# Group B's decoded attention: operands held as plain fp32, values computed with 64 stationary columns of one key head

## The chip, the cores and the metric

The kernel runs on one core of one Trainium2 chip. The metric is the device time of one execution in microseconds (us). The time before is 2622.76 us, the median of three runs (2622.56 to 2625.93).

The engines are named as in the profile: PE is TensorE, the matrix engine (PEld its weight loads), DVE VectorE, ACT ScalarE, POOL GpSimd, SP SyncE, which here only issues transfers. "L207" is line 207 of the kernel.

## The reference

One layer of an encoder that serves a prompt of 512 frames and, in the same step, 8 decoded sequences (batches) of 16 new frames each. The normed input goes through one combined projection, whose columns belong to two groups of attention heads, A and B. The change touches group B of the decoded batches, and nothing else. Cut to that:

```python
DEC_BATCH, DEC_SEQ, HEAD_DIM = 8, 16, 64
N_HEADS_B, N_KV_B, GQA_R, B_WINDOW = 16, 2, 8, 128

def band_attend(q, k, v, valid, bias=None, sink=None):
    s = jnp.einsum('bgqhrd,bgkhd->bghrqk', q, k) * (HEAD_DIM ** -0.5)
    ...
    m = jnp.max(s, axis=-1, keepdims=True)
    m = jnp.maximum(m, sink)
    p = jnp.exp(s - m)
    denom = jnp.sum(p, axis=-1, keepdims=True) + jnp.exp(sink - m)
    o = jnp.einsum('bghrqk,bgkhd->bgqhrd', p / denom, v)
    ...

def sample_layer(x, ck_a, cv_a, ck_b, cv_b, ...):
    ...
    ob = band_attend(qb.reshape(b, 1, s, N_KV_B, GQA_R, HEAD_DIM),
                     jnp.concatenate([ck_b, kb], axis=1)[:, None],
                     jnp.concatenate([cv_b, vb], axis=1)[:, None],
                     jnp.ones((1, keep_b + s), dtype=bool), sink=sinks.reshape(N_KV_B, GQA_R))
```

For each batch there are 16 query heads over 2 key heads (8 query heads to each), 16 query frames, and 128 cached keys with 16 new ones behind them. So for one batch and one key head the scores are a matrix of 128 (8 heads times 16 frames) by 144 (128 cached and 16 new keys), with 64 numbers summed in each product; the values are 128 by 64, summed over 144 keys. Each row of the scores goes through a softmax with a sink, an extra term in the denominator.

## The kernel before, in words

**Precision.** The output is compared in fp32. A large product is computed as three matmuls in the fp32r format (`mm3`, lines 207 to 209): each operand is split into a rounded part hi and the rest lo, and hi·hi, hi·lo and lo·hi are summed in one bank of PSUM. `split` makes the two parts: ScalarE rounds (line 198), VectorE subtracts (line 199). Small products, as the reciprocal norm's broadcast (line 263), are single matmuls in plain fp32. One such matmul stands in the profile as two PE instructions.

**The stream of projections.** `dense` computes a block of 128 output features for 640 frames: for each of 16 feature tiles of the input, and each half of 320 frames, one `mm3` into a bank named `dn`. In the trace these are the rows "L207 PE MATMUL dn<-S,W 128x320" and so on; they run nearly all the time. Their weights come in by SP's queue (line 219) and are split by ScalarE and VectorE as tiles W of 128 by 1024.

**Attention is woven in.** Attention is written as generators (functions with `yield`). After each feature tile `dense` calls `tick` (line 96), which adds `rate` to a counter and for each whole one runs one piece, up to the next `yield`, of the streams in turn. From the fifth pair of heads on the two streams are the prompt's heads of group A and "decode", and the rate is 1.1. "decode" holds `decode_b` (group B, this change), and after it `decode_a(0)` (half of group A). The scheduler then orders each engine's instructions by when it expects them to be ready; a few constraints keep the order of the projections, of the slots' uses and of some pieces. So what a piece issues stands among projection matmuls, and how many stand between two pieces is the scheduler's choice.

**Memory slots.** Tiles on chip take slots from lists: S (62 slots), W (12), and D, 10 slots set aside for decoding. A slot's next user waits for its last reader. PSUM holds four `bank()` tiles (named `at`), which prompt and decode share.

**`decode_b` before (lines 584 to 644).** Queries and keys lie with features on the partitions: rows 0 to 63 belong to key head 0, rows 64 to 127 to key head 1. For each half of four batches:
- it loads cached keys, cached values and this half's queries into three S slots (lines 589 to 591). The queries come from a DRAM scratch `sb_d`, written after rotation (rope, lines 560 and 561 its four small transfers for each tile);
- it splits queries, keys and values into six D slots, and POOL copies the 16 new keys of each batch, hi and lo, behind the cached ones (line 600);
- for each batch, and for each of the two key heads, an `mm3` on the key head's 64 rows gives the scores, 128 by 144, in a bank. The softmax follows: VectorE's row maximum (615), the sink (616), POOL's memset (619), ScalarE's exponentials (620, 621), and VectorE's denominator, reciprocal and products (622 to 625), which give the probabilities: 128 for the cached keys and 128 for all batches' new keys, zero but for this batch's 16;
- after two yields `flip` transposes the four blocks of probabilities (line 324, four matmuls into one bank) and splits the bank into two S slots;
- one piece later two `mm3` of 128 stationary columns (both key heads' values) by 256 moving columns (both key heads' probabilities) give the values, the first against the cache, the second against the new frames `vb_own`, kept as hi and lo. Of the 128 by 256 result two quarters of 64 by 128 are wanted; VectorE copies them (line 638).

Then the result is written out, and `decode_a(0)` takes its turn.

## Time and profile before

| what | value |
|---|---|
| median of three runs | 2622.76 us |
| span of the profiled execution, first to last instruction | 2619.7 us |
| what stands outside that span, against the median | 3.1 us |
| mean granted clock of TensorE | 0.997 |
| busy, PE / VectorE / ScalarE / POOL | 2565.2 / 2027.7 / 1101.9 / 663.8 us |
| `decode_b` on TensorE, first scores to last values | about 405 to 480 us |

Busy time is the sum over an engine's instructions. A matmul's record overlaps that of the next one, so the cost of one is read from start to start. A row of the timeline gives the start, the duration, engine, line, operation and tiles, the number of instructions run together, and in brackets how long the engine waited and for what. A group's row gives the busy sum and the mean in ns of one, then the idle time ahead of it. A window's row gives the window, its length, the busy time (and count) of PE, PEld, VectorE, ScalarE and POOL, the granted clock, the share of the transfers and GB/s.

### The profile page before, as it was taken

How to read it: one execution, taken by the hardware profiler on the slowest of the kernel's cores; microseconds unless marked ns; L12 is line 12 of the kernel's file. 1: busy time of each engine (PE TensorE's matmuls, PEld its weight loads, DVE VectorE, ACT ScalarE, POOL GpSimd, SP SyncE). 2: the span in 40 equal slices, each digit the busy share in tenths (PEclk: the TensorE clock that was granted, in tenths of full speed). 3: DMA queues.
4: the chain of work that ended last, by engine and by line, in shares of the span. 5: the costliest groups of instructions: out<-in, count | busy, mean ns of one | idle time of the engine just before them, and what ended most of it. 6: DMA issues, size and time to landing. Idle time of an engine off the chain costs nothing.

```text
span 2619.7 us, 45100 instructions
## 1 busy us (share of the span) xinstructions
PE 2565.2 (98%) x17437; PEld 2527.9 (96%) x17437; DVE 2027.7 (77%) x3133; ACT 1101.9 (42%) x1797; POOL 663.8 (25%) x573
## 2 busy tenths in 40 slices
PE   8999999999999999999999999999999899999997
PEld 8999998999899999999999999999999899999996
DVE  5775676766866888788888888888888877777797
ACT  5553444444633644443433333433434333333343
POOL 0000000000301203332333333323324433333353
PEclk9999999999999999999999999999999999999998
DMA  5322232444655433443343343343445865666655
GB/s 172 101 69 91 94 102 86 133 124 130 214 188 185 155 131 122 160 162 126 131 142 126 130 144 123 131 146 120 133 147 176 280 189 157 175 175 169 192 156 176
DMA packets 178678, 383.87 MB, mean 147 GB/s; under 512 B 21856, under 2 KB 74080, under 8 KB 178464
## 3 DMA queue, kind: packets, MB, share of 16 engines
q1 hardware_dynamic: 154128, 326.92, 38.8%
q0 software_dynamic: 23184, 52.77, 7.1%
q8 instruction: 137, 2.24, 0.3%
q10 hardware_dynamic: 1152, 1.31, 0.1%
q14 instruction: 77, 0.63, 0.1%
HBM read 299.61 MB, written 80.58 MB: 145 GB/s over the span
## 4 chain that ended last, share of the span: by engine, by line
PE 85%; DVE 8%; DMA 3%; ACT 2%; issue 2%; POOL 0%; SPq 0%; DVEq 0%; ACTq 0%; POOLq 0%
PE dn L209 18%; PE dn L207 18%; PE dn L208 18%; PE at L207 9%; PE at L208 9%; PE at L209 9%; DVE W L199 2%; PE at L324 2%; DMA W<-w_down 1%; PE at L419 1%; DVE S L973 1%; ACT W L198 1%; PE at L215 1%; PE at L214 1%; ACT S L440 0%
## 5 line engine op out<-in xcount | busy, mean ns | idle before, releaser
L207 PE MATMUL dn<-S,W 128*128 128x320 f32 x3694 | 1152.5, 312 | 5.2 <-ACT S L1027 2.7
L209 PE MATMUL dn<-S,W 128*128 128x320 f32 x3694 | 1144.5, 310 | 6.7 <-DVE W L199 6.3
L208 PE MATMUL dn<-S,W 128*128 128x320 f32 x3694 | 1143.3, 310 | 2.0 <-DVE S L203 1.7
L198 ACT ACTIVATE W<-W 128x1024 fp32r<-128x1024 f32 (+2 forms) x632 | 608.2, 963 | 965.9 <-PE dn L208 542.8
L199 DVE TENSOR_TENSOR W<-W,W 128x1024 fp32r<-128x1024 f32 (+2 forms) x632 | 738.7, 1169 | 81.5 <-ACT W L198 77.6
L209 PEld LDWEIGHTS dn<-S,W 128*128 128x128 f32 x3694 | 694.1, 188 | 10.5 <-DVE W L199 10.1
L207 PEld LDWEIGHTS dn<-S,W 128*128 128x128 f32 x3694 | 694.7, 188 | 9.0 <-ACT S L1027 3.0
L208 PEld LDWEIGHTS dn<-S,W 128*128 128x128 f32 x3694 | 694.4, 188 | 4.1 <-DVE S L203 1.9
L209 PE MATMUL at<-S,W 128*128 128x320 f32 x1594 | 493.5, 310 | 4.9 <-DVE W L199 4.8
L207 PE MATMUL at<-S,W 128*128 128x320 f32 x1594 | 492.8, 309 | 0.5 <-ACT W L198 0.5
L208 PE MATMUL at<-S,W 128*128 128x320 f32 x1594 | 492.5, 309 | 0.0
L954 POOL TENSOR_TENSOR W<-W,W 128x1024 f32<-128x1024 f32 (+2 forms) x75 | 158.9, 2118 | 637.5 <-DVE W L199 453.6
L209 PEld LDWEIGHTS at<-S,W 128*128 128x128 f32 x1594 | 299.2, 188 | 7.3 <-DVE W L199 7.3
L207 PEld LDWEIGHTS at<-S,W 128*128 128x128 f32 x1594 | 299.3, 188 | 0.8 <-ACT W L198 0.8
L208 PEld LDWEIGHTS at<-S,W 128*128 128x128 f32 x1594 | 299.3, 188 | 0.0
L973 DVE TENSOR_TENSOR S<-S,dn 128x320 f32<-128x320 f32 x358 | 163.8, 480 | 65.4 <-PE dn L209 65.0
L963 POOL TENSOR_TENSOR W<-W,W 128x1024 f32<-128x1024 f32 (+2 forms) x75 | 163.6, 2181 | 118.9 <-DVE W L199 113.5
L949 DVE TENSOR_TENSOR W<-W,W 128x1024 f32<-128x1024 f32 (+2 forms) x76 | 124.6, 1640 | 62.8 <-DMA W<-w_down 29.5
L973 DVE TENSOR_TENSOR S<-S,at 128x320 f32<-128x320 f32 x262 | 123.3, 480 | 51.4 <-PE at L209 50.5
L980 POOL DMA_DIRECT2D S<-act_d x161 | 88.0, 547 | 178.6 <-PE dn L209 92.0
L951 DVE TENSOR_TENSOR W<-W,W 128x1024 f32<-128x1024 f32 (+2 forms) x76 | 83.4, 1097 | 61.6 <-DMA W<-w_up 31.4
L1044 DVE TENSOR_TENSOR S<-S,half 128x320 fp32r<-128x320 f32 x147 | 120.0, 837 | 1.9
(162 smaller groups left out, 2223.3 us busy)
## 6 DMA issues: line engine op xcount, KB each, us to landing
S<-act_d POOLq DMA_DIRECT2D x161, 320.0 KB, 3.7
W<-w_gate SPq DMA_DIRECT2D x88, 512.0 KB
W<-w_up SPq DMA_DIRECT2D x88, 512.0 KB
W<-w_in SPq DMA_DIRECT2D x66, 512.0 KB
W<-w_down SPq DMA_DIRECT2D x64, 384.0 KB
act_d<-half SPq DMA_DIRECT2D x147, 160.0 KB
act_d<-S SPq DMA_DIRECT2D x147, 160.0 KB
W<-w_down SPq DMA_DIRECT2D x68, 320.0 KB
```

The source lines that it names most:

```text
L198: self.nc.scalar.activation(hi, src, AF.Identity)
L199: self.nc.vector.tensor_tensor(lo, src, f(hi), ALU.subtract)
L207: mm(out, a[0], b[0], start=first, stop=False)
L208: mm(out, a[0], b[1], start=False, stop=False)
L209: mm(out, a[1], b[0], start=False, stop=last)
L949: nc.vector.tensor_tensor(b12[:, w], b12[:, w], b22[:, w], sub)
L951: nc.vector.tensor_tensor(s6[:, w], b11[:, w], b12[:, w], sub)
L954: eng.tensor_tensor(b11[:, w], b22[:, w], s6[:, w], sub)
L963: eng.tensor_tensor(b21[:, w], b21[:, w], s6[:, w], sub)
L973: add = lambda o, a, b: nc.vector.tensor_tensor(o, a, b, ALU.add)
L980: nc.gpsimd.dma_start(out=r(sh(t, 2, HT)), in_=r(act_d[which, :, j]))
L1044: nc.vector.tensor_tensor(r(src), src, hi, ALU.subtract)
```

## The change

Queries, keys and values of decoded group B are no longer split; they lie as plain fp32 in one D slot each, and every product is a plain fp32 matmul.

- Keys: the load goes straight into the D slot, into 128 of each batch's 144 columns, and POOL puts hi + lo of the new keys behind them. Values: the load goes straight into a D slot. Queries: loaded into an S slot as before; POOL copies them into the D slot in the order that the matmul reads. The new frames' values, `vn`, are hi + lo, added by POOL once.
- Scores: one matmul for each key head, on its 64 rows; both are issued before the two softmaxes.
- Transposes: the same four, in the order of key heads; ScalarE copies the bank into one S slot, and there is no subtraction.
- Values: four matmuls, for cache and new frames and each key head, with 64 stationary columns of that key head by its 128 moving columns. The results lie at rows 0 to 63 and 64 to 127 of one bank of 128 columns; VectorE copies them at once.

```diff
-            kraw, vraw, qraw = n.get("S"), n.get("S"), n.get("S")
-            dma(out=sh(kraw, 4, CB), in_=io["ckb"][:, 4 * hf:4 * hf + 4])
-            dma(out=sh(vraw, 4, P), in_=io["cvb"][:, 4 * hf:4 * hf + 4])
+            ko, vo, qo = (n.get("D") for _ in range(3))
+            qraw = n.get("S")
+            k, v, q = sh(ko, 4, CB + DS), sh(vo, 4, P), sh(qo, 4, P)
+            dma(out=k[:, :, :CB], in_=io["ckb"][:, 4 * hf:4 * hf + 4])
+            dma(out=v, in_=io["cvb"][:, 4 * hf:4 * hf + 4])
             dma(out=sh(qraw, 8, 64), in_=sb_d[:, :, 64 * hf:64 * hf + 64])
-            yield
-            qo, ko, vo = [(n.get("D"), n.get("D")) for _ in range(3)]
-            ...
-            n.split(sh(qraw, 8, 64).rearrange("p t (b s) -> p b t s", b=4), *qd)
-            n.split(sh(kraw, 4, CB), kd[0][:, :, :CB], kd[1][:, :, :CB])
-            for e in range(2):
-                ...
-                nc.gpsimd.tensor_copy(kd[e][:, :, CB:], src)
-            n.split(sh(vraw, 4, P), *vd)
-            n.put("S", kraw, vraw, qraw)
+            new = [f(x)[:, 64 * hf:64 * hf + 64].rearrange("p (b s) -> p b s", b=4) for x in kb_own]
+            nc.gpsimd.tensor_tensor(k[:, :, CB:], *new, ALU.add)
+            if hf == 0:
+                vn = n.get("D")
+                nc.gpsimd.tensor_tensor(vn[:, :P], f(vb_own[0]), f(vb_own[1]), ALU.add)
+            yield
+            nc.gpsimd.tensor_copy(sh(qo, 4, 8, DS), sh(qraw, 8, 64).rearrange("p t (b s) -> p b t s", b=4))
+            n.put("S", qraw)
             yield
             ...
-                    qq = [qd[e][rows, bb].rearrange("p t s -> p (t s)") for e in range(2)]
-                    n.mm3(ps, qq, (kd[0][rows, bb], kd[1][rows, bb]), True, True)
+                    nc.tensor.matmul(ps, q[rows, bb], k[rows, bb], start=True, stop=True)
             ...
-                own, pt2 = flip([pts[0][1][:, :P], pts[1][1][:, :P], pts[0][1][:, P:], pts[1][1][:, P:]], "S")
+                ps = n.bank()
+                for i, (_, pt) in enumerate(pts):
+                    for x in range(2):
+                        tr(ps[:, P * (2 * x + i):P * (2 * x + i) + P], pt[:, P * x:P * x + P])
                 n.put("S", *(t for t, _ in pts))
+                pt2 = n.get("S")
+                nc.scalar.activation(pt2[:, :4 * P], ps, AF.Identity)
                 yield
-                po = n.bank()[:, :256]
-                n.mm3(po, (vd[0][:, bb], vd[1][:, bb]), cut(pt2, 0, 256), True, False)
-                n.mm3(po, vb_own, cut(pt2, 256, 512), False, True)
-                n.put("S", *own)
-                for j in range(2):
-                    ...
-                    nc.vector.tensor_copy(o_s[rows, :, DS * b:DS * b + DS],
-                                          po[rows, P * j:P * j + P].rearrange("p (t s) -> p t s", t=8))
+                po = n.bank()[:, :P]
+                for x, vv in enumerate((v[:, bb], vn)):
+                    for j in range(2):
+                        nc.tensor.matmul(po[64 * j:64 * j + 64], vv[:, 64 * j:64 * j + 64],
+                                         pt2[:, P * (2 * x + j):P * (2 * x + j) + P], start=x == 0, stop=x == 1)
+                n.put("S", pt2)
+                nc.vector.tensor_copy(o_s[:, :, DS * b:DS * b + DS], po.rearrange("p (t s) -> p t s", t=8))
                 yield
```

In the rows of order that follow, `dn` is a projection's bank, `at` one of the four others, S, W and D-list slots are tiles with running numbers (a D slot still has the name of the S slot it was), and a row holds line, operation, output and operands.

TensorE at the first batch's scores, before:

```order
L209 MATMUL dn_4441<-S_36_145,W_716_4444 128x320
L207 MATMUL at_4531<-S_733_4499,S_731_4497 128x144
L208 MATMUL at_4531<-S_734_4500,S_731_4497 128x144
L209 MATMUL at_4531<-S_733_4499,S_732_4498 128x144
L207 MATMUL at_4548<-S_733_4499,S_731_4497 128x144
L208 MATMUL at_4548<-S_734_4500,S_731_4497 128x144
L209 MATMUL at_4548<-S_733_4499,S_732_4498 128x144
L207 MATMUL dn_4441<-S_39_151,W_715_4443 128x320
```

and with the change (line 609 is the new scores):

```order
L209 MATMUL dn_4441<-S_36_145,W_716_4444 128x320
L609 MATMUL at_4522<-S_720_4465,S_722_4467 128x144
L609 MATMUL at_4524<-S_720_4465,S_722_4467 128x144
L207 MATMUL dn_4441<-S_39_151,W_715_4443 128x320
L208 MATMUL dn_4441<-S_40_152,W_715_4443 128x320
```

Two matmuls stand where six stood, at the same place among the projections.

TensorE in the second half, values of one batch and scores of the next, before:

```order
L207 MATMUL dn_5022<-S_63_199,W_876_5212 128x320
L207 MATMUL at_5244<-S_879_5234,S_849_5091 128x256
L207 MATMUL at_5259<-S_847_5089,S_845_5087 128x144
L208 MATMUL at_5259<-S_848_5090,S_845_5087 128x144
L209 MATMUL at_5259<-S_847_5089,S_846_5088 128x144
L208 MATMUL at_5244<-S_880_5235,S_849_5091 128x256
L209 MATMUL at_5244<-S_879_5234,S_850_5092 128x256
L207 MATMUL at_5244<-S_879_5234,S_6_84 128x256
L208 MATMUL at_5244<-S_880_5235,S_6_84 128x256
L209 MATMUL at_5244<-S_879_5234,S_7_85 128x256
L207 MATMUL at_5276<-S_847_5089,S_845_5087 128x144
L208 MATMUL at_5276<-S_848_5090,S_845_5087 128x144
```

and with the change (line 639 is the new values, x2 the two key heads):

```order
L207 MATMUL dn_4980<-S_51_175,W_862_5143 128x320
L208 MATMUL dn_4980<-S_52_176,W_862_5143 128x320
L209 MATMUL dn_4980<-S_51_175,W_863_5144 128x320
L639 MATMUL at_5100<-S_849_5098,S_835_5031 64x128 x2
L639 MATMUL at_5100<-S_849_5098,S_724_4473 64x128 x2
L609 MATMUL at_5112<-S_834_5030,S_836_5032 128x144
L609 MATMUL at_5114<-S_834_5030,S_836_5032 128x144
L207 MATMUL dn_4980<-S_51_175,W_862_5143 128x320
```

Before, one key head's scores stand inside the value matmuls, behind the first of them; now the values stand together with both key heads' scores behind them. Between the transposes and the values stand, in the second half, five or six projection matmuls (five before), and between a batch's scores and its first two transposes 13 (16 or less before, with values and the other scores among them). The last two transposes follow four projection matmuls later; in the first half the two pairs are up to 19 projection matmuls apart.

SP's queue around the last rope transfers, before (`ckb` and `cvb`, the loads of keys and values, come later there, behind the writes of `ob_d`, `o_ka` and `sa_d`):

```order
L219 DMA W_678_4141<-w_in 128x1024
L560 DMA S_627_3872<-S_626_3870 8x640
L561 DMA S_627_3872<-S_626_3870 8x640
L560 DMA S_627_3872<-S_626_3870 8x640
L561 DMA S_627_3872<-S_626_3870 8x640
L219 DMA W_693_4229<-w_in 128x1024
L767 DMA sb_d<-S_626_3870 128x128
L219 DMA W_703_4318<-w_in 128x1024
```

and with the change (the write of `sb_d` is now line 771):

```order
L219 DMA W_678_4141<-w_in 128x1024
L591 DMA S_720_4465<-ckb 128x4x128
L592 DMA S_721_4466<-cvb 128x512
L560 DMA S_627_3872<-S_626_3870 8x640
L561 DMA S_627_3872<-S_626_3870 8x640
L560 DMA S_627_3872<-S_626_3870 8x640
L561 DMA S_627_3872<-S_626_3870 8x640
L219 DMA W_693_4229<-w_in 128x1024
L591 DMA S_834_5030<-ckb 128x4x128
L592 DMA S_835_5031<-cvb 128x512
L771 DMA sb_d<-S_626_3870 128x128
L219 DMA W_703_4318<-w_in 128x1024
```

Both halves' loads of keys and values moved up, the first ahead of the rope transfers, the second ahead of the write of the queries; with one weight load between them. The queries' loads stay behind that write.

12 lines of the change are left out of this document (5 added, 7 removed).

## The prediction

> **What bounds the kernel now.** I read the page first: busy times and the chain of waits.
>
> ```profile
> span 2619.7 us, 45100 instructions
> PE 2565.2 (98%) x17437; PEld 2527.9 (96%) x17437; DVE 2027.7 (77%) x3133; ACT 1101.9 (42%) x1797; POOL 663.8 (25%) x573
> PE 85%; DVE 8%; DMA 3%; ACT 2%; issue 2%; POOL 0%; SPq 0%; DVEq 0%; ACTq 0%; POOLq 0%
> ```
>
> TensorE is busy for 98% of the span and makes 85% of the chain, so a microsecond taken off its stream, or off a wait of it, is a microsecond of the end; work taken off VectorE, ScalarE or the queues counts only where TensorE waits for it. Decoded group B lies at about 405 to 480 us, woven into the first `dense` products of the second half of the projections. So I read that stretch next: by windows, then the order of time on TensorE.
>
> ```profile
> 415.00:425.00 10.00, 8.75 (x60) 7.57 (x59) 8.45 (x25) 6.71 (x18) 0.00 (x0) 1.00 0.25 80
> 445.00:455.00 10.00, 8.70 (x62) 7.94 (x61) 8.19 (x22) 4.12 (x12) 1.31 (x6) 1.00 0.36 114
> PE at L324 <- DVE S L625: 1.4, 2, 1.1
> ```
>
> The clock is full (1.00), and TensorE still lacks 1.25 and 1.30 us of busy time in two windows of 10 us. It waits there at line 324, the transposes, for the probabilities that VectorE writes (line 625 of the old code: 1.4 us in two waits). Busy time hides a part of such waits, since a matmul's record overlaps the next; therefore I take costs from start to start. A projection matmul of 320 columns steps by 0.147 us.
>
> **Scores, taken apart.** One batch before:
>
> ```profile
> 405.87 0.31 PE L209 MATMUL dn<-S,W 128*128 128x320 f32 x1
> 406.11 0.34 PE L207 MATMUL at<-S,S 64*128 64x144 f32 x2
> 406.28 0.28 PE L208 MATMUL at<-S,S 64*128 64x144 f32 x2
> 406.39 0.28 PE L209 MATMUL at<-S,S 64*128 64x144 f32 x2
> 406.61 0.41 PE L207 MATMUL dn<-S,W 128*128 128x320 f32 x1
> 406.86 0.31 PE L208 MATMUL dn<-S,W 128*128 128x320 f32 x1
> ```
>
> From 405.87 to 406.86 lie two steps of 0.147 and 0.69 us for the scores. In it: 0.09 ahead (406.11 - 405.87 - 0.147) and 0.10 behind (406.86 - 406.61 - 0.147), paid for going to 64 rows and back, and three slots. In each slot two matmuls start together (x2): the program has all three of one key head before the other's, and still the two key heads, on rows 0 to 63 and 64 to 127, run side by side. The change leaves one plain fp32 matmul for each key head. What such a one costs shows in the reciprocal norm's broadcast, which is fp32:
>
> ```profile
> 60.14 0.60 PE L263 MATMUL at<-cst,sm 128*128 128x128 f32 x4
> L263 PE MATMUL at<-cst,sm x60: 222/275/417, 60.1 to 2606.5; 128*128 128x128 f32 x40, 128*128 128x64 f32 x20
> ```
>
> Six fp32 matmuls for each call make 12 instructions, so one is two passes; four passes take 0.60 us with the last one's 0.275, so a pass steps by (0.60 - 0.275)/3 = 0.11 us at 128 columns, hence about 0.12 at 144. Side by side that is two slots of 0.12 for three of 0.11 (406.28 to 406.39): 0.09 us less for a batch, **-0.7 us** for eight. If the key heads ran one after the other: 4 x 0.12 + 0.19 = 0.67, no gain. I take -0.7, since the same rows run in pairs here.
>
> **Values.** A batch that waits for nothing:
>
> ```profile
> 443.62 0.31 PE L209 MATMUL dn<-S,W 128*128 128x320 f32 x1
> 443.76 0.28 PE L207 MATMUL at<-S,S 128*128 128x256 f32 x1
> 443.88 0.28 PE L208 MATMUL at<-S,S 128*128 128x256 f32 x1
> 444.48 0.31 PE L207 MATMUL dn<-S,W 128*128 128x320 f32 x1
> ```
>
> Six matmuls of 256 columns, 0.72 us, and no switch on either side (443.76 is one step behind 443.62). The change puts four fp32 matmuls there, eight passes of 0.11, each on half of the array's columns. No matmul of before uses half the columns, so I bound it by both ways in which tiles could go. In pairs: 4 x 0.11 + 0.19 for the switch that the scores show = 0.63, 0.09 less, -0.7 us for eight. One after the other: 8 x 0.11 + 0.19 = 1.07, 0.35 more, +2.8 us. I take **-0.7**, the nearest row being the scores' pairs.
>
> The Trainium skill bears on both halves of this: "TensorEngine Tiling (Array Packing)", section Key Properties, has tiles run their weight loads and matmuls in parallel, which would give the lower value, and says that a change of tiling mode drains TensorE, which speaks against a new mode for the values; the 0.09 and 0.10 us around the scores agree. "TensorE: Matmul & The Clock Gate", section "Part 3: Packing small matmuls — row/col tiling", says that matmuls start strictly in program order; by that the eight passes would need five slots instead of four, 0.11 us for a batch or 0.9 us in all more, and the values would gain nothing. The pairs above, which start ahead of their program order, disagree with it.
>
> **Waits for the split.** Before, the flipped probabilities are rounded by ScalarE and their rest taken by VectorE, and the second of the six value matmuls needs the rest.
>
> ```profile
> 455.24 0.31 PE L208 MATMUL dn<-S,W 128*128 128x320 f32 x1
> 455.56 0.65 PE L207 MATMUL at<-S,S 128*128 128x256 f32 x2
> 456.36 0.38 PE L208 MATMUL at<-S,S 128*128 128x256 f32 x1
> 457.62 0.41 PE L209 MATMUL dn<-S,W 128*128 128x320 f32 x1
> 457.87 0.30 PE L207 MATMUL dn<-S,W 128*128 128x320 f32 x1
> 455.54 0.69 DVE L199 TENSOR_TENSOR S<-at,S 128x512 fp32r<-128x512 f32 x1 [1.19 <-ACT S L198]
> L199 DVE TENSOR_TENSOR S<-at,S 128x512 fp32r<-128x512 f32 x12 | 8.1, 688 | 5.3 <-ACT S L198 5.3
> L198 ACT ACTIVATE S<-at 128x512 fp32r<-128x512 f32 x12 | 7.1, 592 | 8.6 <-PE at L324 8.6
> ```
>
> From 455.24 to 457.87 stand, less two steps, 2.34 us in which values and the next scores are done, whose work is 0.72 + 0.69 = 1.41: 0.9 us too many. VectorE's subtraction runs from 455.54 to 456.23, just ahead of the value matmul at 456.36, and the scores, started in between, don't go in pairs. By the same count of starts, the eight batches stand at 0.2, 1.2, 0.3, 0.0, 0.9, 0.9, 0.7 and 0.3 us too many, in all 4.5. With operands unsplit only ScalarE's copy (0.59 us) stands between transposes and values; the subtraction (0.69) and its queue go. What ScalarE still gates stays: 0.1 to 0.2 us ahead of the first value matmul in six batches (455.56 - 455.24 - 0.147 = 0.17), 1.0 in all, and in the second half the values now stand five or six projection matmuls (0.8 us) behind the transposes, less than the copy and the two latencies (0.27 and 0.2) need, 0.2 each. I take **-3.0** (bounds 0, if another wait takes the place, and -4.5).
>
> **Waits of the transposes.**
>
> ```profile
> 451.92 0.31 PE L209 MATMUL dn<-S,W 128*128 128x320 f32 x1
> 453.30 0.30 PE L324 MATMUL at<-cst,S 128*128 128x128 f32 x1 [1.06 <-DVE S L625]
> 421.24 0.31 PE L207 MATMUL dn<-S,W 128*128 128x320 f32 x1
> 422.45 0.55 PE L324 MATMUL at<-cst,S 128*128 128x128 f32 x3 [0.90 <-DVE S L624]
> 449.71 0.34 PE L207 MATMUL at<-S,S 64*128 64x144 f32 x2
> 449.37 0.69 DVE L199 TENSOR_TENSOR S<-S,S 128x512 fp32r<-128x512 f32 x1
> 449.98 1.22 DVE L199 TENSOR_TENSOR W<-W,W 128x1024 fp32r<-128x1024 f32 x1
> 451.12 0.30 DVE L615 TENSOR_REDUCE sm<-at 128x1 f32<-128x144 f32 x1
> ```
>
> TensorE stands 1.23 us at 453.30 and 1.06 at 422.45; with 0.5 at 419.78 and 1.1 in the second half such waits come to 3.8 us. The first one's chain begins late, because VectorE does the last of the second half's three operand splits (0.69 at 449.37) and a weight's subtraction (1.22) before the row maximum at 451.12; the scores, which start at 449.71, were done by 450.3. Without the splits the maximum can start 0.8 us sooner: -0.8. At 422.45 the order now puts 19 projection matmuls, 2.8 us, between the two pairs of transposes, so this wait is covered: -0.8. Against it, in the second half the first transposes now stand 13 projection matmuls behind the start of the scores, 0.5 + 1.9 = 2.4 us; they need 0.5 for the scores and 2.2 from the row maximum to line 625's end (451.12 to 453.30, the transpose itself): 0.3 too little in each of three batches, less 0.5 that these wait by now: +0.4. Sum **-1.2**, bounds -3.8 and, in the last rival, well above zero.
>
> **What I cost at nothing, and its cover.** POOL's copy that reorders the queries and its three sums:
>
> ```profile
> L281 POOL TENSOR_TENSOR S<-S,S 128x640 f32<-128x640 f32 x7 | 12.6, 1804 | 13.7 <-ACT S L280 13.5
> L649 POOL MEMSET S<- 128x640 f32 x2 | 1.2, 634 | 0.0
> 348.53 0.65 SPq L560 DMA_DIRECT2D S<-S  x1
> 378.79 0.42 SPq L589 DMA_DIRECT2D S<-ckb  x1
> 440.64 0.56 SPq L591 DMA_DIRECT2D S<-sb_d  x1
> 343.19 0.40 PE L419 MATMUL at<-S,S 128*128 128x256 f32 x2
> ```
>
> The copy of 512 columns lies between a memset's share of 640 (0.5 us) and a sum's (1.4). The queries' load is issued at 440.64, the scores that need it start at 449.71: 9 us, for the load and the copy. If that cover went, each half would lose up to 1.4 us. The key and value loads move up SP's queue, the first pair ahead of the last rope's four transfers (issued from 348.53 on) and a weight load. They wait for the last reader of their slot, a prompt score matmul that starts at 343.19, so rope is not held; if it were, the weight load behind it would be late. The key load's rows are 512 bytes instead of 2 KB, with 60 us to land (378.79 was the old issue).
>
> **Sum.** -0.7 - 0.7 - 3.0 - 1.2 = -5.6 us. The profiled span is 2619.7, so 2614.1; the runs' median, 2622.76, lies 3.1 us above the span for what stands around it, and the forecast on that scale is **2617.2 us**. Behind the first batches of decoded group A no engine's order changes, and TensorE bounds it, so the gain should reach the end.
>
> **Rivals.** About 0.2%, 5.2 us, is what a measurement tells from no change here: below 2617.5 is faster.
> (a) Everything waits less: all of 4.5 and 3.8 goes; -0.7 - 0.7 - 8.3 = -9.7, 2613.1. For it: VectorE loses about 16 subtractions or copies of 0.69 in 70 us. Against it: softmax and weight splits stay in front of the probabilities. Chance 0.14.
> (b) Column halves run one after the other: +3.5 on the forecast (2.8 and the 0.7 not won), 2620.7. For it: no row shows column tiles; against it, the row tiles. Chance 0.15.
> (c) The wait changes its owner: weights' splits on ScalarE and VectorE (1.22 us at 449.98) hold the copy and the probabilities as the subtraction did, and only the work is saved: -1.4, 2621.4. Chance 0.13.
> (d) Slower: the transposes' new places are too early. If a batch waits as at 453.30 and again as at 422.45, 2.3 us each, the waits exceed the 3.8 of before plus the 4.4 otherwise won (0.7 + 0.7 + 3.0) from 3.6 batches on; at five it is 11.5 - 8.2 = +3.3, 2626.1. For it: 0.3 us too little cover even undisturbed. Against it: the prompt softmax that delayed 422.45 comes once. Chance 0.08.
> That the change does not do what it says, that the fp32 passes do not pair, is (b) with the scores' 0.7 added, 2621.4.
>
> **How the numbers follow.** The forecast keeps 0.50, its own range 2615.2 to 2619.2 (the -3.0 and the -1.2 uncertain by one each). Somewhat over half of that, 0.28, and (a) and a little of the others' edges are faster by over 0.2%: 0.45. Slower by over 0.2% (above 2628.0) needs (d) at six batches or more: 0.05. Within: 0.50. The range from 2612.9 to 2623.4 takes in (a), (b), (c) and leaves out (d).
>
> **What would show it.** Scores: two pairs, then the next projection matmul 0.4 us behind their start (0.5 now). Values: starts in pairs, first projection matmul about 0.54 us behind; eight single starts would be (b). No projection or value matmul waiting for VectorE between transposes and values. Busy time in 445 to 455 above 9.3. Transposes that wait over 1 us in more than three batches would be (d). What would make the forecast wrong first is the pairing of columns, and after it how many of the waits move to the probabilities.

## The result, and the profile after

| | median us | runs | span of the profiled execution |
|---|---|---|---|
| before | 2622.66 | 6 (2621.72 to 2627.99) | 2619.7 |
| the change | 2614.12 | 6 (2611.41 to 2616.59) | 2614.7 |

The ratio is 0.9965, with a 95% interval of 0.9953 to 0.9976: faster by 0.35%, or 8.5 us. The forecast was 2617.2, a gain of 5.6.

The same rows of the page as before the change (span, busy times, the chain by engine), and the two windows that stood there with 1.25 and 1.30 us missing:

```profile
span 2614.7 us, 45074 instructions
PE 2563.0 (98%) x17437; PEld 2526.7 (97%) x17437; DVE 2015.7 (77%) x3111; ACT 1098.1 (42%) x1791; POOL 664.2 (25%) x574
PE 87%; DVE 6%; DMA 3%; issue 2%; ACT 2%; POOL 0%; SPq 0%; DVEq 0%; ACTq 0%; POOLq 0%
415.00:425.00 10.00, 9.80 (x72) 8.79 (x72) 8.73 (x26) 6.60 (x17) 0.00 (x0) 1.00 0.27 93
445.00:455.00 10.00, 9.96 (x72) 8.69 (x71) 5.52 (x19) 3.67 (x12) 0.20 (x1) 1.00 0.40 130
```

TensorE's busy time fell by 2.2 us only, VectorE's by 12.0 (2027.7 before). The two windows now lack 0.20 and 0.04 us. So the gain is waiting that went, and it went in this stretch. To measure that apart from what happens in the other 2500 us, I take two marks which every version has, and read them from start to start. The first mark is VectorE's taking of a projection's result (line 394), first and last of the six such in the stretch; the second is the first row that the feed-forward part reads back and splits (line 1044 before). In these rows stand count, duration in ns (least, median, most), and the start of the first and the last in us. Before:

```profile
L394 DVE TENSOR_TENSOR S<-dn,S x6: 814/824/825, 398.8 to 509.4; 128x640 f32<-128x640 f32 x6
L1044 DVE TENSOR_TENSOR S<-S,half x147: 476/483/2705, 1006.6 to 2007.5; 128x320 fp32r<-128x320 f32 x147
```

and after:

```profile
L394 DVE TENSOR_TENSOR S<-dn,S x6: 816/824/825, 398.7 to 502.1; 128x640 f32<-128x640 f32 x6
L1048 DVE TENSOR_TENSOR S<-S,half x147: 476/485/2707, 999.6 to 2000.2; 128x320 fp32r<-128x320 f32 x147
```

The stretch from the first to the last of the six took 110.6 us before (509.4 - 398.8) and 103.4 after: **-7.2 us**. To the second mark it is 607.8 and 600.9, -6.9. Behind about 490 us the order of every engine is the same in both programs, so what comes later is execution. In the profiled execution 2 us were lost again at the very end: the same projection matmul came 7.0 us earlier than before at 2571 us and 5.05 us earlier at 2600. There a single wait of TensorE for a weight that VectorE splits lasts 1.8 us instead of 0.6 (one of its rows of waits in the last 80 us: total, times, longest; before, and then after), and behind it the granted clock is 0.83 in ten microseconds, where it was 1.00 before:

```profile
PE at L209 <- DVE W L199: 1.2, 3, 0.6
```

```profile
PE at L209 <- DVE W L199: 2.4, 3, 1.8
2573.00:2583.00 10.00, 9.65 (x55) 9.65 (x56) 9.93 (x16) 3.30 (x5) 3.86 (x2) 0.83 0.33 98
```

The spans of the changed kernel's other executions lie between 2609.6 and 2614.8, so the profiled one is at the long end of a spread of 5 us. That is why the profile's spans differ by 5.0 us and the medians by 8.5.

**Scores** of the first batch. TensorE in order of time, the two key heads' two passes each as one row:

```profile
405.75 0.31 PE L209 MATMUL dn<-S,W 128*128 128x320 f32 x1
405.99 0.52 PE L609 MATMUL at<-S,S 64*128 64x144 f32 x4
406.44 0.41 PE L207 MATMUL dn<-S,W 128*128 128x320 f32 x1
406.69 0.31 PE L208 MATMUL dn<-S,W 128*128 128x320 f32 x1
```

From 405.75 to 406.69, less two steps of 0.147, is 0.64 us; before it was 0.69. The single starts are 405.990 and 405.997, then 406.217 and 406.224: in pairs, as forecast, but the first slot lasts 0.23 us and not 0.12.

**Values** of the same batch:

```profile
412.12 0.31 PE L209 MATMUL dn<-S,W 128*128 128x320 f32 x1
412.36 0.66 PE L639 MATMUL at<-S,S 128*64 128x128 f32 x8
412.95 0.42 PE L207 MATMUL dn<-S,W 128*128 128x320 f32 x1
413.20 0.31 PE L208 MATMUL dn<-S,W 128*128 128x320 f32 x1
```

From 412.12 to 413.20, less two steps, is 0.785 us, more than the 0.72 of before. The eight passes start in four pairs (412.361, 412.521, 412.630, 412.740, each with its partner 7 ns later). In the second half the scores of the next batch follow at once:

```profile
452.34 0.31 PE L209 MATMUL dn<-S,W 128*128 128x320 f32 x1
452.58 0.66 PE L639 MATMUL at<-S,S 128*64 128x128 f32 x8
453.17 0.52 PE L609 MATMUL at<-S,S 64*128 64x144 f32 x4
453.62 0.42 PE L207 MATMUL dn<-S,W 128*128 128x320 f32 x1
453.87 0.31 PE L208 MATMUL dn<-S,W 128*128 128x320 f32 x1
```

Both together cost 453.87 - 452.34 - 0.29 = 1.23 us, which is 0.19 less than 0.785 + 0.64: the two groups share one switch of tiles, so that the 0.09 ahead and the 0.10 in the first projection step behind are paid once. Nothing in the row of values or scores waits; before, the same two groups took 2.34 us (455.24 to 457.87).

**Transposes.** TensorE's waits from 395 to 485 us (total, times, longest) have one row for them, and these are its two waits:

```profile
PE at L324 <- DVE S L623: 0.4, 2, 0.2
421.82 0.31 PE L207 MATMUL dn<-S,W 128*128 128x320 f32 x1
422.33 0.47 PE L324 MATMUL at<-cst,S 128*128 128x128 f32 x2 [0.20 <-DVE S L623]
428.68 0.38 PE L324 MATMUL at<-cst,S 128*128 128x128 f32 x2
429.28 0.47 PE L324 MATMUL at<-cst,S 128*128 128x128 f32 x2 [0.23 <-DVE S L623]
```

By starts the first stands 0.36 us too long (422.33 - 421.82 - 0.147). The second, between the two pairs of the next batch, stands 0.38 too long (429.28 - 428.68 less two transposes of 0.11); nothing waited there before the change. The eight batches together wait 1.8 us; before it was 3.8. (Two expectations below write 1.45 for it: that sum lacks the wait at 429.28.)

Counted in the same way over all eight batches (costs from start to start, less the projection's steps):

| us | before | after | |
|---|---|---|---|
| scores, nothing waiting, 8 x | 0.69 | 0.64 | -0.4 |
| values, nothing waiting, 8 x | 0.72 | 0.785 | +0.5 |
| switch shared by values and scores, 4 x | - | -0.19 | -0.8 |
| waits inside values and scores | 4.5 | 0.15 | -4.35 |
| waits of the transposes | 3.8 | 1.8 | -2.0 |
| sum | | | -7.0 |

The marks say -7.2.

### The profile page after: what moved, and what is told of

Same layout as the page of the kernel before. It is cut to its first block, busy times and chain, and to the rows that moved or that the text cites. A ratio compares the mean times of both kernels' runs of the same rounds, so it can differ in the third digit from the quotient of the medians.

```text
span 2614.7 us, 45074 instructions
## 1 busy us (share of the span) xinstructions
PE 2563.0 (98%) x17437; PEld 2526.7 (97%) x17437; DVE 2015.7 (77%) x3111; ACT 1098.1 (42%) x1791; POOL 664.2 (25%) x574
## 4 chain that ended last, share of the span: by engine, by line
PE 87%; DVE 6%; DMA 3%; issue 2%; ACT 2%; POOL 0%; SPq 0%; DVEq 0%; ACTq 0%; POOLq 0%
PE dn L209 18%; PE dn L207 18%; PE dn L208 18%; PE at L207 9%; PE at L208 9%; PE at L209 9%; DVE W L199 2%; PE at L324 2%; DMA W<-w_down 2%; PE at L419 1%; DVE S L977 1%; PE at L215 1%; PE at L214 1%; ACT W L198 1%; ACT S L440 0%
```

## The experiments

Twelve versions were run. All times are read at the marks and counted from the first one. The versions reach that between 397.4 and 398.8 us; these differences arise ahead of decoded group B, so they are taken out. The expectations were written as shifts against the kernel before without that correction, which changes them by 0.1 to 1.3 us.

| version | first to last of the six | to the second mark | ratio of times, 95% |
|---|---|---|---|
| before | 110.6 | 607.8 | 1 |
| the change | 103.4 (-7.2) | 600.9 (-6.9) | 0.9965 (0.9953 to 0.9976) |
| scores only | 105.3 (-5.3) | 606.8 (-1.0) | 0.9981 (0.9971 to 0.9992) |
| values only | 107.1 (-3.5) | 604.2 (-3.6) | 0.9984 (0.9975 to 0.9994) |
| wide values | 105.5 (-5.1) | 605.5 (-2.3) | 0.9976 (0.9967 to 0.9985) |
| copy on VectorE | 103.6 (-7.0) | 604.5 (-3.3) | 0.9970 (0.9959 to 0.9982) |
| old order of transposes | 103.1 (-7.5) | 602.7 (-5.1) | 0.9979 (0.9968 to 0.9989) |
| head by head | 103.5 (-7.1) | 601.8 (-6.0) | 0.9972 (0.9961 to 0.9982) |
| before, spaced | 107.6 (-3.0) | 615.9 (+8.1) | 1.0037 (1.0023 to 1.0051) |
| change, spaced | 103.6 (-7.0) | 613.0 (+5.2) | 1.0018 (1.0009 to 1.0028) |
| joined | 106.2 (-4.4) | 606.2 (-1.6) | 0.9988 (0.9979 to 0.9997) |
| joined and spaced | 103.0 (-7.6) | 601.7 (-6.1) | 0.9977 (0.9968 to 0.9986) |
| joined, rate 1.2 | 111.4 (+0.8) | 607.5 (-0.3) | 0.9995 (0.9986 to 1.0004) |
| rate 1.3 | 109.8 (-0.8) | 605.3 (-2.5) | 0.9993 (0.9984 to 1.0002) |

The first six versions below the change have its order on every engine behind some 500 us. For them the ratio follows the first column within 2 us (scores only: -5.3 there, and 0.9981 is -5.0 us; values only: -3.5 and -4.2; copy on VectorE: -7.0 and -7.9). The second column is one execution, and up to 4.3 us of it go between the marks although the order doesn't differ there (up to 3.4 us, in the copy on VectorE, where the slots of the tiles are the change's as well).

The last six have their pieces of work at other places, so the first column compares unequal work there. Counted by instructions and priced by their steps in the traces, an estimate, TensorE has 1.2 us less to do between the first and the last of the six in each spaced version than in the version without the extra yield, and against the change 1.3 less in joined and spaced, 2.6 more in joined, 6.3 more in joined at rate 1.2 and 5.8 more at rate 1.3. Up to the second mark all versions have done the same work, but for the arithmetic of `decode_b` itself.

The waits of TensorE in decoded group B, in us and counted as in the table before, in the versions on which the argument rests:

| version | inside values and scores | transposes | both |
|---|---|---|---|
| before | 4.5 | 3.8 | 8.3 |
| the change | 0.15 | 1.8 | 2.0 |
| scores only | 2.3 | 1.6 | 3.9 |
| values only | 1.1 | 4.3 | 5.4 |
| before, spaced | 0.9 | 6.3 | 7.2 |

### Scores alone

```diff
-            ko, vo, qo = (n.get("D") for _ in range(3))
+            ko, qo = (n.get("D") for _ in range(2))
+            vraw, qraw = n.get("S"), n.get("S")
...
+            n.split(sh(vraw, 4, P), *vd)
...
+                own, pt2 = flip([...], "S")
+                n.mm3(po, (vd[0][:, bb], vd[1][:, bb]), cut(pt2, 0, 256), True, False)
+                n.mm3(po, vb_own, cut(pt2, 256, 512), False, True)
```

> Scores, queries and keys as in the changed kernel (plain fp32); values as before the change: cached values split, flipped probabilities split, six value matmuls of 128 by 256. All times are against the kernel before, at the projection whose result VectorE takes (line 394) at 509.41 us before and 502.1 us after the change (-7.3).
> Theory (the waits are those of the value matmuls for the split's rest on VectorE, and of the transposes behind VectorE): the wait for the rest stays in most batches, so of the -5.0 us won in scores and values at most 1.5 come; the transposes, relieved of two of three operand splits, win 0.5 to 2. In all -1 to -3 us.
> Rival (the load taken off VectorE and ScalarE anywhere does it, in proportion): the change removes 6 operand splits and 8 flipped ones; this keeps 2 and 8, so about a third of the gain, -2.4, spread over both kinds of wait, and the waits within the value group shrink by a third.
> Rival (fewer passes on TensorE do it): -0.4 us.

Measured: -5.3 us. All three expectations fell; the theory by the most instructive amount, since the split that was to hold TensorE is all there. One batch of the second half, on TensorE:

```profile
L394 DVE TENSOR_TENSOR S<-dn,S x6: 811/822/825, 398.2 to 503.5; 128x640 f32<-128x640 f32 x6
452.83 0.35 PE L207 MATMUL at<-S,S 128*128 128x256 f32 x1
453.11 0.52 PE L609 MATMUL at<-S,S 64*128 64x144 f32 x4
454.53 0.28 PE L208 MATMUL at<-S,S 128*128 128x256 f32 x1
```

The first value matmul and the scores stand where they stood. But the order has now put six projection matmuls between the scores and the value matmul that needs the rest (453.11 to 454.53), and that one waits for nothing. In the second half's batches there are 6, 1 and 2 projections at that place, and in none of them does the matmul that needs the rest wait; the one long wait left is 0.55 us at 422.54, for ScalarE's rounding. So at the values it was not the split as such that cost time but the distance: its reader stood too close behind it. The transposes wait 1.6 us here, as little as after the change, so what they won comes with the scores' half of the change.

### Values alone

```diff
-            n.split(sh(vraw, 4, P), *vd)
+            dma(out=v, in_=io["cvb"][:, 4 * hf:4 * hf + 4])
...
             n.split(sh(qraw, 8, 64).rearrange("p t (b s) -> p b t s", b=4), *qd)
             n.split(sh(kraw, 4, CB), kd[0][:, :, :CB], kd[1][:, :, :CB])
...
                     n.mm3(ps, qq, (kd[0][rows, bb], kd[1][rows, bb]), True, True)
```

(Queries, keys and scores as before the change, but both key heads' scores are issued ahead of the two softmaxes; the rest as in the change.)

> Values as in the changed kernel (plain fp32, 64 stationary columns of one key head, probabilities copied by ScalarE, no rest); scores as before: queries and keys split into two parts, six score matmuls of 64 rows.
> Theory: the wait for the rest is gone, and scores no longer fall inside the value group: -4 to -5.5 us at the mark for scores and values, less 0.4 for the dearer scores than after the change; the transposes win less than after the change since VectorE still does four of six operand splits: 0 to -1.5. In all -4 to -6.5.
> Rival (load in proportion): 2 operand and 8 flipped splits go of 14: about -5 us; not told apart by the sum, but the wait at the second half's first transposes (1.23 us before, 0.2 after) would then fall by two thirds, where the theory leaves it over 0.8.
> Rival (fewer passes): +0.5 us.

Measured: -3.5 us, half a microsecond short of the theory's range. The waits in the value group are gone but for one of 0.93 us, for ScalarE's copy. What holds the gain back is the transposes, 4.3 us of waits in all. The second half's first ones wait 0.38 us, which is what the rival of the load had said and not the theory (over 0.8). But the next two batches wait 1.0 and 1.4, without an operand split of their own in front, so the load in proportion doesn't fit either. The last of these, TensorE and ScalarE:

```profile
L394 DVE TENSOR_TENSOR S<-dn,S x6: 819/825/825, 398.1 to 505.2; 128x640 f32<-128x640 f32 x6
463.42 0.41 PE L324 MATMUL at<-cst,S 128*128 128x128 f32 x2 [1.27 <-DVE S L630]
461.18 0.63 ACT L198 ACTIVATE S<-S 128x512 fp32r<-128x512 f32 x1 [2.48 <-DMA S<-sa_d]
```

At 461.18 ScalarE splits an operand of group A, whose transfer it had waited for (2.48 us, `sa_d`); the exponential of this batch, whose maximum was ready at 460.5, stood behind it until 461.72. After the change the same split runs at 460.48 and waits for nothing. So this wait of the transposes is a collision, of the chain from row maximum to probabilities (some 2.2 us) with one piece of other work, here an operand of group A whose transfer came late. Scores and values alone win 5.3 and 3.5 us, together 7.2: each part moves the others' places.

### Values with 128 stationary columns

```diff
-                for x, vv in enumerate((v[:, bb], vn)):
-                    for j in range(2):
-                        nc.tensor.matmul(po[64 * j:64 * j + 64], vv[:, 64 * j:64 * j + 64], ...)
+                for x, vv in enumerate((v[:, bb], vn[:, :P])):
+                    nc.tensor.matmul(po, vv, pt2[:, 256 * x:256 * x + 256], start=x == 0, stop=x == 1)
```

> As the changed kernel, but the values with both key heads' 128 stationary columns by both key heads' 256 moving columns: two plain fp32 matmuls instead of four on half the columns; VectorE copies two quarters as before the change.
> Theory: four passes of 256 columns at about 0.22 us, no switch of tiles ahead and behind: 0.88 us for a batch against 0.785 with column halves standing alone (0.69 where scores follow at once, where the switch moves over to the scores and saves nothing now). So +0.1 us a batch, +0.8 in all, and +0.8 where the shared switch is lost in four batches: -5.7 to -6.9 us at the mark against before. The value group shows no wait for VectorE.
> Rival (the column halves are what wins): the gain falls by more than half, to above -3.5.

Measured: -5.1 us, 0.6 less than the theory's range. The price of the group was right:

```profile
L394 DVE TENSOR_TENSOR S<-dn,S x6: 816/820/825, 398.7 to 504.2; 128x640 f32<-128x640 f32 x6
412.21 0.31 PE L209 MATMUL dn<-S,W 128*128 128x320 f32 x1
412.36 1.02 PE L638 MATMUL at<-S,S 128*128 128x256 f32 x4
413.03 0.50 PE L207 MATMUL dn<-S,W 128*128 128x320 f32 x1
413.37 0.30 PE L208 MATMUL dn<-S,W 128*128 128x320 f32 x1
```

413.37 - 412.21 - 0.29 = 0.87 us, four passes of 256 columns at some 0.2. Against 0.785 that is 0.6 us over eight batches, and the shared switches are worth 0.8. The other 0.7 are waits: about 1 us more inside values and scores, a little less at the transposes (1.6). So the 64 stationary columns bring 1.4 us by their price and 2.1 as measured, a fifth to three tenths of the gain and not over half of it. Against the six split matmuls (0.72) neither form of fp32 is cheaper on TensorE.

### VectorE copies the probabilities

```diff
-                nc.scalar.activation(pt2[:, :4 * P], ps, AF.Identity)
+                nc.vector.tensor_copy(pt2[:, :4 * P], ps)
```

> As the changed kernel, but VectorE instead of ScalarE copies the flipped probabilities out of the bank; one instruction moved to the other queue, TensorE's work the same.
> Theory (what costs is standing in VectorE's queue between transposes and values): the copy queues behind weight subtractions of 1.2 us and softmax steps, so value matmuls wait again in three or more batches: 1 to 3.5 us are lost of the 7.3, -4 to -6 at the mark, unless the order moves the values further back.
> Rival (only the amount of work counts, not the queue): within 0.5 us of the changed kernel.

Measured: -7.0 us, as the rival said. A copy in VectorE's queue costs nothing here:

```profile
L394 DVE TENSOR_TENSOR S<-dn,S x6: 803/825/825, 398.4 to 502.0; 128x640 f32<-128x640 f32 x6
451.49 0.69 DVE L634 COPY S<-at 128x512 f32<-128x512 f32 x1 [0.42 <-PE at L324]
```

It starts 0.42 us behind the transposes, takes 0.69, and a weight's subtraction follows. In two batches the order has moved the values further back (12 and 11 projection matmuls behind the last transposes instead of 5 and 6). That is the exception that the theory had named, so this run alone doesn't decide between the two. In the batch shown the values stand six projection matmuls behind the transposes, ten after the change, and still wait for nothing. So standing in VectorE's queue is not enough for a wait.

### The old order of the transposes

```diff
-                for i, (_, pt) in enumerate(pts):
-                    for x in range(2):
+                for x in range(2):
+                    for i, (_, pt) in enumerate(pts):
                         tr(ps[:, P * (2 * x + i):P * (2 * x + i) + P], pt[:, P * x:P * x + P])
```

> As the changed kernel, with the four transposes of a batch in the order of before (both key heads' cached part first, then the new frames' parts), nothing else. The order of TensorE then has one transpose, 5 projection matmuls and three transposes in the second half (before and with only scores changed: the same), instead of two, 4 and two.
> Theory (less work in front of the probabilities on VectorE shortens the transposes' waits, not their order): within 0.6 us of the changed kernel, -6.7 to -7.9 at the mark; waits at the transposes 1.0 to 2.0 in all (1.45 after the change).
> Rival (the new order of the transposes earns the 2.35 us that these waits lost): they come back, -5.0 to -5.5 at the mark.

Measured: -7.5 us, waits of the transposes 1.85, against 1.8 after the change. The order in which the four are issued does not matter here.

### One key head's values after the other

```diff
-                for x, vv in enumerate((v[:, bb], vn)):
-                    for j in range(2):
+                for j in range(2):
+                    for x, vv in enumerate((v[:, bb], vn)):
```

> As the changed kernel, but the program issues both value matmuls of one key head (cache, new frames) before those of the other: four passes on the left half of the columns, then four on the right.
> Theory (halves of the columns run side by side ahead of the program's order, as the row halves of before did): starts still in pairs, 0.78 us for a batch that waits for nothing; within 0.5 us of the changed kernel.
> Rival (column halves run together only when they follow each other in the program): 7 or 8 single slots of 0.10, 1.1 to 1.2 us a batch, 2.5 to 3.3 us lost, -4 to -4.8 at the mark.

Measured: -7.1 us. The first batch's values, eight passes:

```profile
411.36 0.66 PE L639 MATMUL at<-S,S 128*64 128x128 f32 x8
```

All eight start within 0.66 - 0.27 = 0.39 us (a single one's record is 0.27), as in the changed kernel; one after the other they would need seven steps of 0.10. A batch costs 0.79 us. The two starts of a pair lie 13 ns apart instead of 7. The halves of the columns run side by side even where the program has all four passes of one half ahead of the other's; the built program keeps that order on TensorE, so it isn't the scheduler that mixed them.

### More distance, without a change of arithmetic

```diff
                 n.put("S", *(t for t, _ in pts))
                 yield
+                yield
                 po = n.bank()[:, :256]
```

(in the kernel before, between transposes and values)

> The kernel before, with one more yield between transposes and values of each batch: no arithmetic changes, only the distance in the stream of projections. Since more pieces of work are needed, the order is another up to about 985 us, so it is compared there too, where the changed kernel stands at -7.0 us.
> Theory (the excess of 4.5 us in the value groups is lack of distance between the split and the matmul that reads it): 2 to 4 us of it go, with the operands as they were; the transposes' waits stay, 3 to 4 us. -2 to -4 us.
> Rival (it is the amount of splitting on VectorE): nothing is won, -0.5 to +1, since the splits are all there.

```profile
L394 DVE TENSOR_TENSOR S<-dn,S x6: 818/823/825, 397.6 to 505.2; 128x640 f32<-128x640 f32 x6
L1045 DVE TENSOR_TENSOR S<-S,half x147: 475/483/2702, 1013.5 to 2014.8; 128x320 fp32r<-128x320 f32 x147
445.94 0.30 PE L324 MATMUL at<-cst,S 128*128 128x128 f32 x1 [1.21 <-DVE S L625]
```

Measured: -3.0 at the first mark (about -1.8 on equal work), and +8.1 at the second. By starts the waits inside values and scores fall from 4.5 to 0.9 us, with every split there as before: that term of the theory holds. The other fell: the transposes wait 6.3 us and not 3 to 4 (1.4 at 445.94), so that of the 8.3 us of waits 7.2 are still there. Distance clears the waits at the values; most of what it wins there is lost again at the transposes. What comes behind the first mark is another matter, and the next run shares it:

```diff
                 yield
                 yield
+                yield
                 ps = n.bank()
```

(in the changed kernel, between softmax and transposes)

> The changed kernel with one more yield between a batch's softmax and its transposes. The order is another up to about 985 us.
> Theory (what is left of the transposes' waits, 1.45 us, is lack of distance): they fall under 0.5 us, 1 us is won, -8.0 at 985 us against -7.0 of the changed kernel.
> Rival (a batch of decoding that takes longer pushes the later pieces, so that group A's waits grow): nothing won or a loss of up to 3 us, to be seen behind 500 us.

```profile
L394 DVE TENSOR_TENSOR S<-dn,S x6: 817/822/825, 397.9 to 501.5; 128x640 f32<-128x640 f32 x6
L1049 DVE TENSOR_TENSOR S<-S,half x147: 475/482/2708, 1010.9 to 2011.7; 128x320 fp32r<-128x320 f32 x147
```

Measured: -7.0 and +5.2. The transposes' waits didn't fall (some 2.7 us), so the theory fell; the rival was right that the loss lies behind 500 us, but it is larger than it said. The two spaced versions lose 11 and 12 us between the marks, 10 and 11 on equal work, nearly all of it from 620 to 730 us (projection matmuls counted one by one). There the last projections from the input end. Whatever decoding is unfinished is then pumped with no projection to weave it into, before group B's operands are built. Counted in the program as it is built, that takes 34 pumps in the kernel before and in the changed one, and 42 in the two spaced versions.

### Fewer pieces, or faster ones

If pieces left over make the loss, giving the eight back must undo it. Values and the next batch's scores in one piece:

```diff
                 nc.vector.tensor_copy(o_s[:, :, DS * b:DS * b + DS], po.rearrange("p (t s) -> p t s", t=8))
-                yield
+                if bb == 3:
+                    yield
```

> The changed kernel with the yield behind the values taken out in all but the last batch of each half: a batch's values and the next batch's scores are one piece. The program itself then has 18 pumps of unfinished decoding left when the last projection is done (34 in the kernel before, in the changed one, 42 with one more yield a batch); those run with no projection to be woven into. Compared at about 985 us, where the changed kernel stands at -7.0.
> Theory (each pump left over costs what the last runs show for eight of them, 11.8 us, 1.5 us each, as long as TensorE stands idle there): TensorE was idle for about 5 us between 640 and 700 us after the change, so between 3 and 12 us more are won, and another 0.8 us from four shared switches: -10 to -19 at 985 us.
> Rival (the loss of the spaced kernels came from the longer distance itself): no gain from fewer pieces, -6 to -8 at 985 us.

> The changed kernel with one more yield between softmax and transposes (as in the slower run with that yield alone) and with values and next scores joined: 34 pumps left over, as many as in the changed kernel.
> Theory (pieces left over made the spaced kernel slower, not the distance): the loss of 11.8 us is gone; -6 to -9 at 985 us.
> Rival (the distance itself, by the later pieces' waits): +0 to +5 at 985 us, as with the yield alone.

```profile
L394 DVE TENSOR_TENSOR S<-dn,S x6: 823/824/826, 398.2 to 504.4; 128x640 f32<-128x640 f32 x6
L394 DVE TENSOR_TENSOR S<-dn,S x6: 812/824/825, 397.8 to 500.8; 128x640 f32<-128x640 f32 x6
L1050 DVE TENSOR_TENSOR S<-S,half x147: 475/481/2702, 999.5 to 2000.7; 128x320 fp32r<-128x320 f32 x147
```

With the same distance and 34 pumps left over, the spaced version stands at -7.6 and -6.1: the loss is gone, and the second expectation's theory holds. But fewer than 34 bring nothing: joined alone, 18 left, is at -4.4 and -1.6, short of both of its expectations. At the first mark that is no loss (2.6 of the 2.8 us against the change are work done earlier); at the second it is. Counted by projection matmuls it is at -4 at 618 us, at -11 at 706 and at -3 from 828 on: what is not done at 650 us is done later, in group A's second half. The last two raise the rate (`n.rate = 1.1`, to 1.2 with the pieces joined and to 1.3 without), so that no pump is left over:

> Values and next scores joined, and the rate of pieces from the fifth pair of heads on 1.2 instead of 1.1: no pump is left over when the projections end.
> Theory (pieces left over): better than with 18 left, by up to 18 x 1.5 us if TensorE stood idle for that long; the idle time between 640 and 700 us bounds it: -10 to -16 at 985 us.
> Rival (pieces that come faster wait more for each other, as their own chain of 2.2 us from row maximum to probabilities stays): what is won at 650 us is lost between 400 and 620 us: -3 to -7 at 985 us.

> The changed kernel with the rate of pieces 1.3 instead of 1.1, nothing else: no pump is left over.
> Theory (pieces left over): -9 to -16 at 985 us.
> Rival (denser pieces wait for each other): the stretch to 620 us loses 3 to 8 us against the changed kernel's -7.3, so that -2 to -7 stands at 985 us.

```profile
L394 DVE TENSOR_TENSOR S<-dn,S x6: 811/824/825, 397.4 to 508.8; 128x640 f32<-128x640 f32 x6
L394 DVE TENSOR_TENSOR S<-dn,S x6: 815/821/825, 398.1 to 507.9; 128x640 f32<-128x640 f32 x6
```

Measured: +0.8 and -0.3, -0.8 and -2.5. Both theories fell. At the second mark rate 1.3 lies in its rival's range; at rate 1.2 with joined pieces the loss was larger than even the rival said. But the rivals' mechanism, that denser pieces wait for each other between 400 and 620 us, is only a small part of what the traces show. The stretch from the first to the last of the six, after the change and at rate 1.3:

```profile
398.66:502.07 103.41, 102.77 (x728) 94.28 (x727) 72.47 (x226) 53.52 (x139) 5.05 (x19) 1.00 0.33 105
398.14:507.88 109.74, 109.18 (x768) 99.81 (x767) 78.87 (x245) 59.17 (x151) 8.29 (x28) 1.00 0.36 111
```

At rate 1.3 the stretch is 6.3 us longer, holds 40 more instructions of TensorE, and lacks 0.56 us of busy time where it lacked 0.64. By the estimate above 5.8 us are pieces done there instead of later, and 6.3 of the 7.9 us at rate 1.2. What remains for waits is about 0.5 and 1.6 us (up to 620 us, by the same estimate, 1.3 and 3.0). Where these versions lose the rest, 4 to 7 us against the change at the second mark, stays open. The price of a piece left over (some 1.3 us, from eight of them on equal work) holds upwards only; fewer of them win nothing. No version here is shown to beat the change.

## Why the prediction was right, and where it was not

The time lay inside the range, 3 us below the forecast. By the 0.2% that the text took as the bound it is faster, which had 0.45, a little less than no change had. By its own steps:

- **That TensorE bounds, and only its stream counts:** right. VectorE lost 12.0 us of work, TensorE 2.2, and the time followed TensorE's waits.
- **Scores, -0.7:** -0.4. The pairs were right. A slot of plain fp32 was priced at 0.12 us from the norm's broadcast; the first one takes 0.23 with 64 rows and 128 stationary columns. The slot is the part of this term that was mis-sized.
- **Values, -0.7:** +0.5, the wrong sign. The pairs of column halves, which no row of before showed, came; rival (b) is out, by the run of one head after the other too. The error was the switch: I took 0.19 us from the scores (0.09 ahead, 0.10 behind), and overlooked that the last slot is longer as well (412.74 to 412.95 is 0.21 and not 0.11), and the first (0.16). My own rows had it: the three slots of the scores before last 0.17, 0.11 and 0.22 us (406.11, 406.28, 406.39, 406.61). With these the switch costs 0.36 us instead of 0.19, and the values come to 0.80; 0.785 was measured.
- **What I had not counted:** where values and scores follow each other, one switch serves both, 0.19 us in four batches, -0.8. So the two terms that were to bring -1.4 brought -0.7, by another way.
- **Waits for the split, -3.0 (bounds 0 and -4.5):** -4.35, nearly the whole. The cause that I gave was too narrow. With this split left in (scores only) the matmuls that need the rest don't wait in the second half, and 2.3 us remain; with one more yield and all splits in place the 4.5 us fall to 0.9. So these waits were a matter of the distance between the split and its reader in the order: the change removed the reader that was too close, and moving it away clears them too. But distance alone didn't win the time: in that spaced version the transposes wait 2.5 us more, and 7.2 us of waits are left where the change leaves 2.0.
- **ScalarE's gate, 1.0 us that were to stay, and 0.2 a batch in the second half:** 0.15 remained. Part of the 0.1 to 0.2 us ahead of the first value matmul is now the switch itself, which stands there anyway.
- **Transposes, -1.2:** -2.0. The second half's first batch did as worked out: the row maximum came 0.86 us earlier behind its scores (0.55 us at 447.15 to 447.70, 1.41 before), and TensorE waited 0.20 for 1.23. The 0.3 us of cover that were to be lacking in each of three batches came as 0.28, 0.20 and nothing, about as worked out. What I left out is that such waits end elsewhere too (0.40 at 454.27 and 0.32 at 467.07 before, 0.08 and nothing now); the batch at 422.33, which I thought fully covered, still waited 0.36, and the next one, for which I had counted nothing, 0.38 at 429.28.
- **At nothing:** the cover held. POOL's copy of the queries waits 0.45 us for the load and is done 6 us ahead of the scores at 447.15; the key load left SP at 342.98, and rope's first transfer followed at 348.06, 0.5 us earlier than before:

```profile
440.32 0.61 POOL L600 COPY S<-S 128x512 f32<-128x512 f32 x1 [0.45 <-DMA S<-sb_d]
342.98 0.40 SPq L591 DMA_DIRECT2D S<-ckb  x1
348.06 0.67 SPq L560 DMA_DIRECT2D S<-S  x1
```

- **Rivals:** (a), all waits go, was nearest: of 8.3 us of waits 6.3 went. (c), that the weights' splits take over as the owner, is out for the values, and may live on in the transposes' 1.8. (d) didn't come with the change, but it is what the values alone show in two batches (waits of 1.0 and 1.4), so it was a fair risk.

So the forecast of 5.6 us was near the 7.2 at the mark by errors that partly cancel: 0.7 too much for TensorE's own work, 2.1 too little for waits. That much of the agreement is luck, and the range, 10.5 us wide, was generous. The medians' 8.5 us is not told apart from 7.2: the interval of the ratio runs from 6.3 to 12.3 us.

What stays open: why the order comes out as it does in each version. The scheduler's estimates aren't in the trace; that distance clears the waits at the values is shown by the spaced version, that the scheduler misjudged the split's end is only argued. Why the transposes' waits grow there and fall with the scores' half of the change is argued too, from the operand splits that no longer stand in front of the probabilities; no run moves those splits alone. Nor is it settled why versions of the same order lose up to 4 us between 500 and 1000 us in their profiled executions. The granted clock dips there in some of them (from 780 to 800 us it was 0.91 with scores only, 1.00 after the change) and goes part of the way.

## What to carry to other kernels

In a stream woven by a scheduler, ask of each wait whether it is the work or the distance: here the value matmuls lost 4.5 us with their reader of the split close behind it, and 0.9 with it one piece further on, the splits being the same. Then look where the time goes instead: 2.5 us of it came back at the transposes. Cheaper arithmetic beside the bounding engine pays when it shortens a chain that something on that engine reads, and the sum of two such changes (5.3 and 3.5 alone, 7.2 together) can't be had from the parts. Distance isn't free either: pieces that no longer fit beside the main stream run bare at its end, 10 to 11 us for eight of them. And compare two versions only between points up to which they have done the same work: a stretch that is 6 us longer may hold 6 us more of it.

## What the runs showed of the hardware that was not expected

- Halves of the array's columns run side by side, even if the program has all four passes of one half first: a batch of eight fp32 passes of 128 columns takes 0.785 us with the halves in turn (pairs 7 ns apart) and 0.79 with one half first (13 ns apart).
- A switch to half rows or half columns and back costs 0.3 us and a little more here: 0.09 ahead, 0.10 in a longer last slot, 0.10 in a longer first projection step, and the first slot is longer too. Going from column halves straight to row halves pays the 0.09 ahead and the first projection step once (1.23 us for both groups, 1.43 apart).
- The first pair of fp32 passes on 64 rows with 128 stationary columns takes 0.23 us, the first pair of passes with 64 stationary columns 0.16; the two pairs that follow in the values 0.11 each.
- Four fp32 passes of 256 moving columns with 128 stationary ones take 0.87 us, more than six fp32r matmuls of the same size (0.72): unsplit fp32 saved no time on TensorE in the values of this kernel.
